# Scattering one expert's output in eight pieces between the next expert's products, and the rotary key's low part as two zero-padded planes

## The chip, the cores and the metric

The kernel runs on one core of a Trainium2 chip. The metric is the device time of one execution in microseconds (us); the time of a version is the median of its runs. One execution is also recorded by the profiler; its span runs from the first to the last instruction.

## The reference

One layer of a transformer block on 512 tokens of width 1024, all in f32:

```python
h   = rmsnorm(x) * (1 + sc1) + sh1                       # shift and scale from a condition vector
c_q, c_kv, k_pe, dil, gates = split(h @ w_in)
o_a = mla_attention(...)     # 8 heads; score = q_nope . k_nope (128 wide) + q_pe . k_pe (64 wide, rotary, one key for all heads)
o_b = dilated_band_attention(...)                        # 3 groups of 8 heads, softmax-weighted
x   = x + gt1 * ((g_a * o_a + g_b * o_b) @ w_out)
h2  = rmsnorm(x) * (1 + sc2) + sh2
aff = softmax(h2 @ w_router)                             # 16 experts
gate, idx = top_k(aff.T, 64)                             # each expert chooses 64 tokens
for each expert e:
    xe  = h2[idx[e]]                                     # 64 x 1024
    ye  = (silu(xe @ w_gate[e]) * (xe @ w_up[e])) @ w_down[e] * gate[e]     # 1024 -> 2048 -> 1024
    out[idx[e]] += ye
x   = rmsnorm(x + gt2 * out)
```

The three matrices of an expert hold 2048 x 1024 f32 each, 8.4 MB; the 16 experts' weights are read once.

## The kernel before

All is one function, `tile_block`. Each engine has its own list of instructions and runs it in order; V is VectorE (DVE), A is ScalarE (ACT), G is GpSimd (POOL), T is TensorE (PE), SP issues nearly all transfers. The program states tiles and operations; a planner (`TileContext(nc, schedule_with_timeline_sim=True)`) sets the order in each list, by the order of the source, but with ready work put ahead where it reckons that an engine would stand still. It adds the waits. A tile name with `bufs=n` has n buffers; a new tile of the name waits until the oldest has been read for the last time. Pools that are closed give their room to later pools, whose first writes wait for the last readers of that room.

Precise products are made from two halves: `split` writes a rounded f32r high part (ACT) and the rest as a low part (DVE, L415 and L416), and three products high x high, high x low, low x high are summed (`TERMS`).

The stages, in order of time:

- Preparation and the projections of the low-rank attention (0 to 126 us). `kr` holds the rotary key: 128 partitions, where two copies of its 64 rows lie one above the other, and two planes, high and low. `ltm`, two 128x128 triangular masks for ranking tokens, is copied here from the masks' tile (L332), and `c32`, the condition vector repeated 32 times, is made here.
- Low-rank attention (126 to 273 us). For each of 4 pairs of heads and 4 blocks of 128 queries, each head's 128x512 scores are five products (L656 to L661): three of `q_` and `k_`, one of `qr` and the high plane of `kr` over 128 rows, and one over 64 rows: `qr` holds a head's query, high part in one half of the partitions and low part in the other, and only the half `r_` with the high part meets the low plane of the key:

```python
T.matmul(pp[hh_], qr[hh_][:, qs], kr[:, 0], start=False, stop=False)           # L660
T.matmul(pp[hh_], qr[hh_][r_, qs], kr[r_, 1], start=False, stop=True)          # L661
```

  Between them lie table lookups (`lookup`, L306 to L330) for the other attention's biases, through DRAM.
- Dilated attention, output projection and routing logits (273 to 921 us), `route` at the end.
- Ranking: the top 64 tokens of each expert (921 to 938 us), mostly on DVE; `ltm` is used at L1055. `onesb` (L1002) is the first tile of the ranking's pool.
- The experts (938 to 1905 us), below, then the last additions, the final norm and the store.

For the experts the weights come through a ring of nine 2 MB buffers (`we`, `RING`). Each expert takes 12 loads: four of `w_gate` and four of `w_up` in turn, each 2 of the 8 blocks of 128 rows, then four of `w_down`. They are issued by SP in that order, each when the buffer that it takes has been read. The last expert's `w_down` comes in smaller column pieces (L990), and one buffer of the ring is used there for the final gains.

For expert e the source goes in this order: `gw`, the one-hot selection of 64 tokens twice side by side (DVE, L1096); `px`, the gathered rows as a product with it (L1101); `xe`, four transposes and scaling to `xT` (L1104 to L1111); transposes of `gw` into `se`, the scatter matrix (L1115, L1117); the gate values `gv` as sums over tokens (L1120); `pg` and `pu`, the products with `w_gate` and `w_up` in four chunks each (L1134); silu and multiplication to `hid` (L1139, L1140), transposed to `hT` (L1143, L1144); `py`, the product with `w_down` (L1151); `yf` and `ye`, scaled and split into high and low (L1155 to L1160); and the scatter: 8 times a product of `se` and `ye` of 512 columns (L1164), added to `x1` by DVE (L1166). `px`, `pg`, `pu` and `py` have 64 rows of output each, in two halves of the 128 partitions side by side ("128*64" in the rows); transposes, sums and scatters use 128 ("128*128").

PSUM has 8 banks: `px` 1, `pg` 2, `pu` 2, `py` 1, and two buffers of `tpb`, which the transposes, the sums and the scatters share.

Of the kernel before, what the change touches and what calls it, by code (L numbers as in the profile page):

```python
# [101 lines left out]
def tile_block(ctx, tc, x, c, positions, w_ada, b_ada, g_norm_mix, w_in, g_q_lat, g_kv_lat, w_uq, w_ukv,  # L102
# [23 lines left out]
    V.memset(one_c, 1.0)  # L126
    a2c = per.tile([P, KD], F32, name="a2c")
    sh2c = per.tile([P, KD], F32, name="sh2c")
    ltm = per.tile([P, 2, P], BF16, name="ltm")

    def axb(E, out_, a, s_, b, op0, op1, t):

# [22 lines left out]
    with ExitStack() as pa:  # L155
# [173 lines left out]
            SP.dma_start(bias_d[u].rearrange("h (a e) k -> a h (e k)", a=16),  # L329
                         stage_d[u].rearrange("(a h) n -> a h n", a=16))  # L330

        V.tensor_copy(ltm, mk[:, M_LT:M_LT + 256].rearrange("p (a n) -> p a n", a=2))  # L332


        th = wk.tile([P, KD], F32, name="cth")
        A.activation(th, cc, AF.Tanh, scale=0.5)
        V.scalar_tensor_tensor(th, th, 1.0, cc, op0=OP.add, op1=OP.mult)
        c32 = hp.tile([P, KD, 32], F32, name="c32")
        V.tensor_scalar(c32, th[:, :, None].to_broadcast([P, KD, 32]), 0.5, None, op0=OP.mult)
        gmix = wk.tile([P, KD], F32, name="gmix")  # L340
        glat = lp.tile([P, 5], F32, name="glat")
# [2 lines left out]
        def ada_step(g, k):  # L344

            load_ada(g, k)
            wt = w_ada_t[g, k]
            if k:
                V.scalar_tensor_tensor(wt, wt, c32[:, k, 0:1], w_ada_t[g, k - 1], op0=OP.mult, op1=OP.add)
            else:  # L350
                V.tensor_scalar(wt, wt, c32[:, k, 0:1], None, op0=OP.mult)

        def ada(g):

# [177 lines left out]
            V.tensor_mul(dst, src, cos)  # L532
            V.tensor_add(dst, dst, t)

        kr = lp.tile([P, 2, S], F32R, name="kr")
        roped(kpe, kpe)
        split(kr, kpe)
        bp_.close()

        st_.close()  # L540
# [94 lines left out]
        for pr_ in range(H // 2):  # L635
            q_, k_, qr, wv4 = cur
            if pr_ == 0:
                vv = values(wv4)
            pT = {}

            def attend(jp):

                po = pj().rearrange("p (h q) -> p h q", h=2)
                for hh_ in range(2):
                    sums(po[:, hh_], [(lambda a, k=k: vv[:, a, k, 128 * hh_:128 * hh_ + 128],
                                       lambda b, k=k: pT[jp, hh_][:, b, k]) for k in range(NT)])
                A.copy(y[:, 2 * pr_:2 * pr_ + 2, 256 * jp:256 * jp + 256], po)

            for j in range(NT):
                place()  # L650
                if j % 2 == 0:
                    for hh_ in range(2):
                        pT[j // 2, hh_] = wk.tile([P, 2, NT, 256], F32R, name="pT", bufs=PTB)
                qs = slice(128 * j, 128 * j + 128)
                pp = [sc(), sc()]
                for hh_ in range(2):  # L656
                    r_ = slice(64 * hh_, 64 * hh_ + 64)
                    for n, (a, b) in enumerate(TERMS):
                        T.matmul(pp[hh_], q_[hh_][:, a, qs], k_[hh_][:, b], start=n == 0, stop=False)  # L659
                    T.matmul(pp[hh_], qr[hh_][:, qs], kr[:, 0], start=False, stop=False)  # L660
                    T.matmul(pp[hh_], qr[hh_][r_, qs], kr[r_, 1], start=False, stop=True)  # L661
                for hh_ in range(2):
                    st4 = wk.tile([P, 4], F32, name="st4", bufs=4)
                    V.reduce_max(st4[:, 0:1], pp[hh_], axis=AX.X)
                    V.tensor_scalar(st4[:, 1:2], st4[:, 0:1], nrs[:, j:j + 1], None, op0=OP.mult)
                    n_pe[0] += 1
                    pe = x1[:, 2 + n_pe[0] // 2 % 2, 512 * (n_pe[0] % 2):512 * (n_pe[0] % 2) + 512]
                    A.activation(pe, pp[hh_], AF.Exp, bias=st4[:, 1:2], scale=prs[:, j:j + 1], accum_out=st4[:, 2:3])
                    V.reciprocal(st4[:, 3:4], st4[:, 2:3])
                    V.tensor_scalar(pe, pe, st4[:, 3:4], None, op0=OP.mult)  # L670
                    pt = tp()
                    for k in range(NT):
                        T.transpose(pt[:, 128 * k:128 * k + 128], pe[:, 128 * k:128 * k + 128], ident)
                    split(pT[j // 2, hh_][:, :, :, 128 * (j % 2):128 * (j % 2) + 128],
                          pt.rearrange("p (k q) -> p k q", k=NT))
                if j == PVJ:
                    attend(0)
                if j == RJ and pr_ < H // 2 - 1:
                    ahead = rope_queries(pr_ + 1)
            if pr_ < H // 2 - 1:  # L680
                cur = project(*ahead)
            attend(1)
            if pr_ < H // 2 - 1:
                vv = values(cur[3])
# [313 lines left out]

        loaded = [weights(0, n) for n in range(len(RING))]

        onesb = wk.tile([P, P], BF16, name="onesb")
        G.memset(onesb, 1.0)  # L1002
        spare = y.rearrange("p h s -> p (h s)")[:, 3 * D:]
# [67 lines left out]
    with ExitStack() as pb_:  # L1071
# [4 lines left out]
        for dh in range(2):  # L1076
            SP.dma_start(gt2[64 * dh:64 * dh + 64],
                         mod_d[5 * D + 512 * dh:5 * D + 512 * dh + 512].unsqueeze(0).to_broadcast([64, 512]))
        for e in range(E_N):
            wl = []  # L1080
            for n in range(12):
# [8 lines left out]
                wl.append(loaded.pop(0) if loaded else weights(e, n))  # L1090
            wg, wu = ([w_.rearrange("p (r f) -> p r f", r=2) for w_ in wl[i:8:2]] for i in range(2))
            wd = [w_.rearrange("p (r d) -> p r d", r=4) for w_ in wl[8:]]

            gw = wbs.tile([P, NT, 2, CAP], F32, name="gw", bufs=1)
            for j in range(NT):
                V.tensor_scalar(gw[:, j], iota[:, None, :].to_broadcast([P, 2, CAP]), pos[:, j, e:e + 1], None,  # L1096
                                op0=OP.is_equal)
            px = ps.tile([P, 512], F32, name="px", bufs=1)
            for j in range(NT):
                for dh in range(2):  # L1100
                    T.matmul(px[64 * dh:64 * dh + 64], gw[:, j, 0], xn[:, j, 512 * dh:512 * dh + 512],  # L1101
                             start=j == 0, stop=j == NT - 1)
            xe = wbs.tile([P, 4, P], F32, name="xe", bufs=1)
            V.tensor_copy(xe, px.rearrange("q (p r) -> q r p", r=4))  # L1104
            pt = ps.tile([P, 512], F32, name="tpb", bufs=2)
            for n in range(4):
                T.transpose(pt[:, 128 * n:128 * n + 128], xe[:, n], ident)
            xT = wbs.tile([P, KD, CAP], F32, name="xT", bufs=2)
            V.tensor_tensor(xT.rearrange("p (h n) s -> p n h s", h=2), pt.rearrange("p (n h s) -> p n h s", n=4, h=2),
                            a2c.rearrange("p (h n) -> p n h", h=2)[:, :, :, None].to_broadcast([P, 4, 2, CAP]), op=OP.mult)  # L1110
            V.tensor_tensor(xT, xT, sh2c[:, :, None].to_broadcast([P, KD, CAP]), op=OP.add)  # L1111

            pt = ps.tile([P, 512], F32, name="tpb", bufs=2)
            for j in range(NT):
# [6 lines left out]
                         start=j == 0, stop=j == NT - 1)  # L1121
            gv = wbs.tile([P, 1], F32, name="gv", bufs=2)
            V.tensor_copy(gv, pt[:, 0:1])

            pg = ps.tile([P, 2, 512], F32, name="pg", bufs=1)
            pu = ps.tile([P, 2, 512], F32, name="pu", bufs=1)
            for c in range(4):
                for w_, acc in ((wg[c], pg), (wu[c], pu)):
                    for r in range(2):
                        k = 2 * c + r  # L1130
                        for b in range(2):
                            for hf in range(2):
                                f0 = 1024 * b + 512 * hf
                                T.matmul(acc[64 * hf:64 * hf + 64, b], xT[:, k], w_[:, r, f0:f0 + 512],  # L1134
                                         start=k == 0, stop=k == KD - 1)
            hid = wbs.tile([P, 2, 4, P], F32, name="hid", bufs=1)
            hT = wbs.tile([P, 4, 4, CAP], F32, name="hT", bufs=1)
            for b in range(2):
                A.activation(hid[:, b], pg[:, b].rearrange("q (p r) -> q r p", r=4), AF.Silu)  # L1139
                V.tensor_mul(hid[:, b], hid[:, b], pu[:, b].rearrange("q (p r) -> q r p", r=4))  # L1140
                pt = ps.tile([P, 512], F32, name="tpb", bufs=2)
                for n in range(4):
                    T.transpose(pt[:, 128 * n:128 * n + 128], hid[:, b, n], ident)  # L1143
# [4 lines left out]
            for g in range(4):  # L1148
                for r in range(4):
                    for dh in range(2):  # L1150
                        T.matmul(py[64 * dh:64 * dh + 64], hT[:, g, r], wd[g][:, r, 512 * dh:512 * dh + 512],  # L1151
                                 start=g == 0 and r == 0, stop=g == 3 and r == 3)

            yf = wbs.tile([P, 512], F32, name="yf", bufs=1)
            V.scalar_tensor_tensor(yf, py, gv, gt2, op0=OP.mult, op1=OP.mult)  # L1155
            ye = wbs.tile([P, 2, 512], F32R, name="ye", bufs=1)
            for dh in range(2):
                r_, o_ = slice(64 * dh, 64 * dh + 64), slice(64 - 64 * dh, 128 - 64 * dh)
                A.activation(ye[r_, dh], yf[r_], AF.Copy)
                V.tensor_sub(ye[o_, dh], yf[r_], ye[r_, dh].bitcast(F32))  # L1160
            for dh in range(2):
                for j in range(NT):
                    pt = ps.tile([P, 512], F32, name="tpb", bufs=2)
                    T.matmul(pt, se[:, j], ye[:, dh], start=True, stop=True)  # L1164
                    ds_ = slice(512 * dh, 512 * dh + 512)
                    V.tensor_add(x1[:, j, ds_], x1[:, j, ds_], pt)  # L1166


        ssf = wbs.tile([P, NT, 3], F32, name="ssf")
# [70 lines left out]
```

## Time and profile before

| | |
|---|---|
| runs | 1934.15, 1939.73, 1940.28 us; median 1939.73 |
| profiled execution | 1937.67 us; span 1935.9 us |
| mean granted TensorE clock | 0.926 of full speed |
| busy share of the span | PE 92%, PE weight loads 55%, DVE 38%, ACT 20%, POOL 8% |
| moved from HBM | 520 MB read, 277 GB/s read and written over the span |

The page gives busy time by engine, the span in 40 slices of 48.4 us with busy tenths, granted clock and DMA share, and the chain of work that ended last. That chain says which instruction, or wait, each stretch of time is owed to. Matmuls are pipelined and their ends are modelled, so the duration of one matmul is longer than the distance to the next; in the chain the rows give the distance.

### The profile page before, as it was taken

To read this page: it belongs to the slowest core of one execution; us is meant where nothing else is said; L and a number is where in the kernel's file an instruction comes from. 1 tells how busy PE (TensorE), PEld (TensorE's weight loads), DVE (VectorE), ACT (ScalarE), POOL (GpSimd) and SP (SyncE) were. 2 spreads that over 40 slices of the span, in tenths; PEclk is the share of its full clock that TensorE was granted. 3 is DMA by queue.
4 is the path that set the end of the run, shared out by engine and by line. 5 is a ranking of instruction groups with operands and counts; after the bars stand their busy time and mean duration, and the time that the engine had idled before them with its cause. 6 is when DMAs were issued, how large, how long until landed. Compare 5 with 4: busy or idle time off the path is not lost.

```text
span 1935.9 us, 21457 instructions
## 1 busy us (share of the span) xinstructions
PE 1777.8 (92%) x8812; PEld 1058.4 (55%) x8812; DVE 739.9 (38%) x1384; ACT 395.4 (20%) x769; POOL 156.0 (8%) x140
## 2 busy tenths in 40 slices
PE   4699999999999999999699999999999999999995
PEld 1466667888888888888233333334333343333332
DVE  6567865556454354445322022211222012220213
ACT  2345643322232322333000000000000000000002
POOL 6710000020020020010200000000000000000002
PEclk7799999999999999999799988899888988889888
DMA  8346666535533234234799999999999999999983
GB/s 268 92 134 212 220 200 199 154 121 154 179 102 119 66 88 122 88 109 177 312 428 427 419 407 406 399 429 403 404 403 424 407 406 406 405 429 405 406 355 93
DMA packets 133537, 531.20 MB, mean 274 GB/s; under 512 B 16952, under 2 KB 93880, under 8 KB 105792
## 3 DMA queue, kind: packets, MB, share of 16 engines
q1 hardware_dynamic: 131360, 523.02, 70.4%
q0 software_dynamic: 2080, 6.82, 0.9%
q8 instruction: 69, 1.13, 0.2%
q14 instruction: 28, 0.23, 0.0%
HBM read 520.45 MB, written 16.17 MB: 277 GB/s over the span
## 4 chain that ended last, share of the span: by engine, by line
PE 84%; DVE 8%; DMA 3%; ACT 2%; issue 2%; SPq 1%; ACTq 0%; DVEq 0%
PE pj L459 20%; PE pg L1134 13%; PE pu L1134 11%; PE py L1151 11%; PE pj L813 5%; PE pj L554 3%; PE px L1101 3%; PE tpb L1164 2%; PE sc L554 2%; DVE x L1166 2%; PE sc L884 1%; PE tpb L1120 1%; DMA raw<-in_w_ada_dram 1%; PE sc L659 1%; DMA y<-in_x_dram 1%
## 5 line engine op out<-in xcount | busy, mean ns | idle before, releaser
L459 PE MATMUL pj<-hh,ws 128*128 128x512 f32 x1248 | 406.4, 401 | 13.7 <-ACT ws L415 8.4
L459 PEld LDWEIGHTS pj<-hh,ws 128*128 128x128 f32 x1248 | 235.7, 189 | 74.4 <-ACT ws L415 8.6
L1134 PE MATMUL pg<-we,xT 128*64 128x512 f32 x1024 | 267.4, 655 | 0.0
L459 PE MATMUL pj<-hl,ws 128*128 128x512 f32 x624 | 249.7, 400 | 3.2 <-DVE hl L449 3.2
L1134 PE MATMUL pu<-we,xT 128*64 128x512 f32 x1024 | 237.3, 592 | 0.0
L1151 PE MATMUL py<-we,hT 128*64 128x512 f32 x960 | 209.3, 594 | 2.6 <-ACT hT L1144 1.1
L416 DVE TENSOR_TENSOR ws<-raw,ws 128x1024 fp32r<-128x1024 f32 (+2 forms) x114 | 141.0, 1239 | 146.7 <-ACT ws L415 146.2
L415 ACT ACTIVATE ws<-raw 128x1024 fp32r<-128x1024 f32 (+2 forms) x114 | 117.0, 1030 | 272.2 <-PE pj L459 188.6
L1134 PEld LDWEIGHTS pg<-we,xT 128*64 128x64 f32 x1024 | 86.2, 151 | 151.8 <-issue 151.5
L1134 PEld LDWEIGHTS pu<-we,xT 128*64 128x64 f32 x1024 | 83.1, 137 | 137.9 <-issue 137.6
L1151 PEld LDWEIGHTS py<-we,hT 128*64 128x64 f32 x960 | 67.6, 137 | 134.6 <-issue 128.5
L459 PEld LDWEIGHTS pj<-hl,ws 128*128 128x128 f32 x624 | 118.1, 189 | 30.5 <-DVE hl L449 3.9
L1164 PE MATMUL tpb<-ye,se 128*128 128x512 f32 x120 | 76.8, 726 | 49.5 <-DVE ye L1160 35.8
L1140 DVE TENSOR_TENSOR hid<-hid,pu 128x512 f32<-128x512 f32 x32 | 20.6, 684 | 243.5 <-PE pu L1134 243.5
L1139 ACT ACTIVATE hid<-pg 128x512 f32<-128x512 f32 x32 | 17.4, 594 | 470.1 <-PE pg L1134 470.1
L1104 DVE COPY xe<-px 128x512 f32<-128x512 f32 x16 | 11.1, 692 | 259.0 <-PE px L1101 259.0
L1155 DVE SCALAR_TENSOR_TENSOR yf<-py,gv,gt 128x512 f32<-128x512 f32 x15 | 11.3, 751 | 221.6 <-PE py L1151 221.6
L813 PE MATMUL pj<-ws,hh 128*128 128x256 f32 x512 | 94.4, 282 | 0.0
L1164 PEld LDWEIGHTS tpb<-ye,se 128*128 128x128 f32 x120 | 31.5, 275 | 100.4 <-issue 59.1
L1166 DVE TENSOR_TENSOR x<-x,tpb 128x512 f32<-128x512 f32 x120 | 78.0, 685 | 14.9 <-PE tpb L1164 13.5
L813 PEld LDWEIGHTS pj<-ws,hh 128*128 128x128 f32 x512 | 79.3, 188 | 0.0
L1101 PE MATMUL px<-xn,gw 128*64 128x512 f32 x256 | 75.8, 613 | 2.0 <-DVE gw L1096 2.0
(331 smaller groups left out, 1941.1 us busy)
## 6 DMA issues: line engine op xcount, KB each, us to landing
we<-in_w_gate_dram SPq DMA_DIRECT2D x64, 2048.0 KB, 15.6
we<-in_w_up_dram SPq DMA_DIRECT2D x64, 2048.0 KB
we<-in_w_down_dram SPq DMA_DIRECT2D x60, 2048.0 KB, 9.3
raw<-in_w_in_dram SPq DMA_DIRECT2D x38, 1024.0 KB, 5.3
raw<-in_w_ada_dram SPq DMA_DIRECT2D x22, 1024.0 KB, 6.9
x<-bkt_d SPq DMA_DIRECT2D x104, 128.0 KB, 4.1
raw<-in_w_in_dram SPq DMA_DIRECT2D x16, 512.0 KB, 5.3
stage_d<-stage POOLq DMA_DIRECT2D x26, 256.0 KB, 4.9
```

The source lines that it names most:

```text
L415: A.activation(dst[:, 0], src, AF.Copy)
L416: V.tensor_sub(dst[:, 1], src, dst[:, 0].bitcast(F32))
L459: T.matmul(pu, parts[k // 4][:, a, k % 4, col:col + 128], hx[b][:, k], start=k == 0 and n == 0, stop=k == KD - 1 and n == 2)
L554: T.matmul(out_, w_(a), b_(b), start=i == 0, stop=i == n_ - 1)
L659: T.matmul(pp[hh_], q_[hh_][:, a, qs], k_[hh_][:, b], start=n == 0, stop=False)
L813: T.matmul(pu[:, 256 * j:256 * j + 256], hx[b][:, k, 128 * m:128 * m + 128], parts[k // 4][:, a, k % 4], start=k == 0 and n == 0, stop=k = ...
L1101: T.matmul(px[64 * dh:64 * dh + 64], gw[:, j, 0], xn[:, j, 512 * dh:512 * dh + 512], start=j == 0, stop=j == NT - 1)
L1134: T.matmul(acc[64 * hf:64 * hf + 64, b], xT[:, k], w_[:, r, f0:f0 + 512], start=k == 0, stop=k == KD - 1)
L1140: V.tensor_mul(hid[:, b], hid[:, b], pu[:, b].rearrange("q (p r) -> q r p", r=4))
L1151: T.matmul(py[64 * dh:64 * dh + 64], hT[:, g, r], wd[g][:, r, 512 * dh:512 * dh + 512], start=g == 0 and r == 0, stop=g == 3 and r == 3)
L1164: T.matmul(pt, se[:, j], ye[:, dh], start=True, stop=True)
L1166: V.tensor_add(x1[:, j, ds_], x1[:, j, ds_], pt)
```

## The change

Two things, with small moves that make room for them.

The scatter of expert e no longer stands at the end of its own pass. Its eight products and additions stand in the pass of expert e + 1, one behind each chunk of `pg` and of `pu`. The transposes of `gw` and the sums for `gv` go behind the products. The next expert's selection and gather (`select`, `gather`) stand between `hid` and its transposes, and the transposes of the gathered rows (`rows`) behind the first quarter of `py`. The first expert has its own ahead of the loop. The last expert's own scatter, which was a separate piece of code, stays as it is.

`kr` gets three planes: the high part, and two low planes with the lower part in one half of the partitions and zeros in the other. The 64-row product becomes one over 128 rows. The zeros are written by GpSimd; the low part is made by two subtractions of 64 partitions.

`ltm` moves to the ranking's pool and is loaded there by a transfer that ACT issues; `c32` moves to a pool that closes earlier, and `ada_step` reads the condition vector from `cc`, which is overwritten with its silu.

```diff
-    ltm = per.tile([P, 2, P], BF16, name="ltm")
-        V.tensor_copy(ltm, mk[:, M_LT:M_LT + 256].rearrange("p (a n) -> p a n", a=2))
...
-        c32 = hp.tile([P, KD, 32], F32, name="c32")
+        V.tensor_scalar(cc, th, 0.5, None, op0=OP.mult)
+        c32 = wk.tile([P, KD, 32], F32, name="c32")
...
-        kr = lp.tile([P, 2, S], F32R, name="kr")
+        kr = lp.tile([P, 3, S], F32R, name="kr")
+        for u in range(2):
+            G.memset(kr[64 - 64 * u:128 - 64 * u, 1 + u].bitcast(F32), 0.0)
         roped(kpe, kpe)
-        split(kr, kpe)
+        A.activation(kr[:, 0], kpe, AF.Copy)
+        for u in range(2):
+            r_ = slice(64 * u, 64 * u + 64)
+            V.tensor_sub(kr[r_, 1 + u], kpe[r_], kr[r_, 0].bitcast(F32))
...
-                    T.matmul(pp[hh_], qr[hh_][r_, qs], kr[r_, 1], start=False, stop=True)
+                    T.matmul(pp[hh_], qr[hh_][:, qs], kr[:, 1 + hh_], start=False, stop=True)
...
+        ltm = wk.tile([P, 2, P], BF16, name="ltm")
+        A.dma_start(ltm.rearrange("p a n -> p (a n)"), masks[:, M_LT:M_LT + 256])
...
+        def select(e): ...      # gw
+        def gather(e, gw): ...  # px
+        def rows(px): ...       # xe, its transposes, xT
+        def scatter(se, ye, j, dh):
+            pt = ps.tile([P, 512], F32, name="tpb", bufs=2)
+            T.matmul(pt, se[:, j], ye[:, dh], start=True, stop=True)
+            ds_ = slice(512 * dh, 512 * dh + 512)
+            V.tensor_add(x1[:, j, ds_], x1[:, j, ds_], pt)
         for e in range(E_N):
...
+            if e == 0:
+                gw = select(0)
+                xT = rows(gather(0, gw))
+            for c in range(4):
+                for i, (w_, acc) in enumerate(((wg[c], pg), (wu[c], pu))):
+                    ...                                  # 8 products
+                    if e:
+                        scatter(se, ye, c, i)
...                                                       # gw transposes to se, gv
...                                                       # hid for b in 0, 1
+            if e < E_N - 1:
+                gw = select(e + 1)
+                px = gather(e + 1, gw)
+            for b in range(2):
...                                                       # hid transposes, hT
...                                                       # py for g in range(4), and in it
+                if g == 0:
+                    xT = rows(px)
...                                                       # yf, ye
-            for dh in range(2):
-                for j in range(NT):
-                    pt = ps.tile([P, 512], F32, name="tpb", bufs=2)
-                    T.matmul(pt, se[:, j], ye[:, dh], start=True, stop=True)
-                    ds_ = slice(512 * dh, 512 * dh + 512)
-                    V.tensor_add(x1[:, j, ds_], x1[:, j, ds_], pt)
```

More of the change, by code (lines that the diff above doesn't have):

```diff
@@ L348, in ada_step @@
             if k:
-                V.scalar_tensor_tensor(wt, wt, c32[:, k, 0:1], w_ada_t[g, k - 1], op0=OP.mult, op1=OP.add)
+                V.scalar_tensor_tensor(wt, wt, cc[:, k:k + 1], w_ada_t[g, k - 1], op0=OP.mult, op1=OP.add)
             else:
-                V.tensor_scalar(wt, wt, c32[:, k, 0:1], None, op0=OP.mult)
+                V.tensor_scalar(wt, wt, cc[:, k:k + 1], None, op0=OP.mult)
         def ada(g):
@@ L656, in tile_block @@
                 for hh_ in range(2):
-                    r_ = slice(64 * hh_, 64 * hh_ + 64)
                     for n, (a, b) in enumerate(TERMS):
@@ L1078, in tile_block, with select, gather, rows @@
                          mod_d[5 * D + 512 * dh:5 * D + 512 * dh + 512].unsqueeze(0).to_broadcast([64, 512]))
+        def select(e):
+            gw = wbs.tile([P, NT, 2, CAP], F32, name="gw", bufs=1)
+            for j in range(NT):
+                V.tensor_scalar(gw[:, j], iota[:, None, :].to_broadcast([P, 2, CAP]), pos[:, j, e:e + 1], None,
+                                op0=OP.is_equal)
+            return gw
+        def gather(e, gw):
+            px = ps.tile([P, 512], F32, name="px", bufs=1)
+            for j in range(NT):
+                for dh in range(2):
+                    T.matmul(px[64 * dh:64 * dh + 64], gw[:, j, 0], xn[:, j, 512 * dh:512 * dh + 512],
+                             start=j == 0, stop=j == NT - 1)
+            return px
+        def rows(px):
+            xe = wbs.tile([P, 4, P], F32, name="xe", bufs=1)
+            V.tensor_copy(xe, px.rearrange("q (p r) -> q r p", r=4))
+            pt = ps.tile([P, 512], F32, name="tpb", bufs=2)
+            for n in range(4):
+                T.transpose(pt[:, 128 * n:128 * n + 128], xe[:, n], ident)
+            xT = wbs.tile([P, KD, CAP], F32, name="xT", bufs=2)
+            V.tensor_tensor(xT.rearrange("p (h n) s -> p n h s", h=2), pt.rearrange("p (n h s) -> p n h s", n=4, h=2),
+                            a2c.rearrange("p (h n) -> p n h", h=2)[:, :, :, None].to_broadcast([P, 4, 2, CAP]), op=OP.mult)
+            V.tensor_tensor(xT, xT, sh2c[:, :, None].to_broadcast([P, KD, CAP]), op=OP.add)
+            return xT
+        def scatter(se, ye, j, dh):
+            pt = ps.tile([P, 512], F32, name="tpb", bufs=2)
+            T.matmul(pt, se[:, j], ye[:, dh], start=True, stop=True)
+            ds_ = slice(512 * dh, 512 * dh + 512)
+            V.tensor_add(x1[:, j, ds_], x1[:, j, ds_], pt)
         for e in range(E_N):
@@ L1092, in tile_block @@
             wd = [w_.rearrange("p (r d) -> p r d", r=4) for w_ in wl[8:]]
-            gw = wbs.tile([P, NT, 2, CAP], F32, name="gw", bufs=1)
-            for j in range(NT):
[L1096 to L1099, printed above, removed]
-                for dh in range(2):
[L1101 to L1104, printed above, removed]
-            pt = ps.tile([P, 512], F32, name="tpb", bufs=2)
[L1106 to L1111, printed above, removed]
+            if e == 0:
+                gw = select(0)
+                xT = rows(gather(0, gw))
+            pg = ps.tile([P, 2, 512], F32, name="pg", bufs=1)
+            pu = ps.tile([P, 2, 512], F32, name="pu", bufs=1)
+            for c in range(4):
+                for i, (w_, acc) in enumerate(((wg[c], pg), (wu[c], pu))):
+                    for r in range(2):
+                        k = 2 * c + r
+                        for b in range(2):
+                            for hf in range(2):
+                                f0 = 1024 * b + 512 * hf
+                                T.matmul(acc[64 * hf:64 * hf + 64, b], xT[:, k], w_[:, r, f0:f0 + 512],
+                                         start=k == 0, stop=k == KD - 1)
+                    if e:
+                        scatter(se, ye, c, i)
             pt = ps.tile([P, 512], F32, name="tpb", bufs=2)
@@ L1123, in tile_block @@
             V.tensor_copy(gv, pt[:, 0:1])
[L1125 to L1135, printed above, removed]
             hid = wbs.tile([P, 2, 4, P], F32, name="hid", bufs=1)
@@ L1140, in tile_block @@
                 V.tensor_mul(hid[:, b], hid[:, b], pu[:, b].rearrange("q (p r) -> q r p", r=4))
+            if e < E_N - 1:
+                gw = select(e + 1)
+                px = gather(e + 1, gw)
+            for b in range(2):
                 pt = ps.tile([P, 512], F32, name="tpb", bufs=2)
@@ L1160, in tile_block @@
                 V.tensor_sub(ye[o_, dh], yf[r_], ye[r_, dh].bitcast(F32))
[L1161 to L1164, printed above, removed]
-                    ds_ = slice(512 * dh, 512 * dh + 512)
-                    V.tensor_add(x1[:, j, ds_], x1[:, j, ds_], pt)
         ssf = wbs.tile([P, NT, 3], F32, name="ssf")
```

## The prediction

> **What bounds the kernel now.** I read the page's slices first, then busy time by stretches, then the chain that ended last.
>
> ```profile
> DMA  8346666535533234234799999999999999999983
> ```
>
> From slice 20 on (950 us, the experts) the DMA engines are full or nearly. Stretches of that stage (columns: stretch, length, busy us of PE, PEld, DVE, ACT, POOL with counts, granted clock, DMA share, GB/s):
>
> ```profile
> 960.00:1060.00 100.00, 92.39 (x409) 33.49 (x405) 20.49 (x35) 7.42 (x13) 0.00 (x0) 0.94 1.01 428
> 1240.00:1250.00 10.00, 9.24 (x26) 5.60 (x28) 6.79 (x15) 0.59 (x1) 0.00 (x0) 0.50 1.00 428
> 1250.00:1260.00 10.00, 10.00 (x40) 3.05 (x38) 0.00 (x0) 0.00 (x0) 0.00 (x0) 0.83 0.75 288
> 951.00:1895.00 944.00, 879.06 (x3717) 348.22 (x3714) 174.56 (x313) 61.70 (x107) 2.45 (x4) 0.90 0.97 408
> 1870.00:1895.00 25.00, 24.14 (x115) 7.86 (x112) 1.03 (x2) 1.08 (x2) 0.00 (x0) 1.00 0.98 336
> ```
>
> PE is busy 879 of 944 and the DMA share is 0.97. A full stream moves 428 GB/s; each expert has one hole (0.75, 288) and, just before it, the clock at 0.50. The chain shows what PE does there, from one expert's last product to the next expert's first ones (start, length, what):
>
> ```profile
> 1222.38 13.98 PE py L1151 x64
> 1236.39 0.76 DVE yf L1155
> 1237.23 0.64 ACT ye L1159
> 1237.89 0.68 DVE ye L1160
> ...
> 1240.90 0.70 DVE x L1166
> 1241.73 0.78 PE tpb L1164
> ...
> 1245.96 0.85 PE tpb L1115 x4
> 1246.82 1.80 PE tpb L1120 x8
> 1248.61 6.02 PE pg L1134 x16
> 1254.63 3.43 PE pu L1134 x16
> ```
>
> Between 1236.36 and 1248.61 PE has 12.25 us of scatter chain, transposes and column sums; it cools, so the first chunk of `pg` takes 6.02 instead of 3.43. No weight slot is released from 1236.4 to 1254.6, the ring of nine runs full, and the queue stands still. So the order on PE sets the end here, and the stream is only 3% behind it: 408 against 428.
>
> **The scatter part: what PE needs.** Products, 8 chunks x 3.43 = 27.4. Scatters, 8 a 512-column fp32r matmul (0.23, row L660 below) plus going from the 128x64 tiling to 128x128 and back. No row shows that pair; the nearest are a one-third-column matmul group among full ones and a 64-row matmul among full ones:
>
> ```profile
> 160.57 1.41 PE tp L324 x24
> 172.15 0.76 PE tp L324 x12
> 184.93 0.70 PE sc L659 x3
> 185.63 0.23 PE sc L660
> 185.86 0.42 PE sc L661
> 186.28 0.89 PE sc L659 x3
> ```
>
> Twelve more of L324 cost 0.65, so 12 at 0.76 hold 0.11 for the visit. L661 takes 0.19 more than L660, and the three behind it 0.19 to 0.20 more than 0.70: 0.39. A visit costs 0.11 to 0.39; I take 0.39, since a scatter changes a full 128-column weight as L661 does. Eight scatters: 0.62 x 8 = 5.0 (2.7 at the other end; below nothing is excluded, it is added work on PE).
> The first scatter stands 3.43 behind the last `py`. Its `ye` needs 0.76+0.64+0.68 and hops, 2.2, the other half 2.9: no wait, 0.5 to spare. Queued behind it is `pu` of the first chunk, and through it the slot release. Each add on DVE (0.70) has a chunk's time, and two `tpb` buffers suffice.
> After the products come the `gw` transposes (0.85) and sums. Warm sums cost 1.05, as in the first expert:
>
> ```profile
> 946.40 1.05 PE tpb L1120 x8
> 947.45 3.58 PE pg L1134 x16
> 1203.78 1.29 PE px L1101 x6
> 1221.00 0.67 PE tpb L1143 x4
> 1221.75 0.59 ACT hT L1144
> ```
>
> They cover the `hid` chain; the next `select` (4 x 0.215 on DVE) stands behind two `hid` multiplies, so `px` starts some 2.65 after the last `pu`, runs 3.43 (16 x 0.215 by the x6 row), then 0.67 and 0.59 until `py`: 7.5 in all. `py` with the `xe` transposes inside (13.98 + 0.67 + 0.39): 15.0; `xT` is ready 10 us before it is wanted. Then the next `pg` at once, warm, 0.2. Sum: 27.4 + 5.0 + 7.5 + 15.0 + 0.2 = 55.1 per expert (52.8 at the cheap end). Today's first `pg` chunks stand 947.45 to 1864.50, over 15 experts 61.1 each.
>
> **What the stream needs.** 0.408 x 944 = 385.2 MB. The last expert's `w_down` (2048 x 1024 x 4 bytes = 8.4 MB, in shorter rows) at 336: 25.0. The other 376.8 MB at 428: 880.4. Together 905.4 instead of 944; a full expert's 25.2 MB (three such matrices) take 58.8. PE's 55.1 is below that, so what was PE's order becomes the stream. SP keeps its order; it waits for slots that are freed in the same order, one every 4.1 instead of 3.43 in the products. The longest stretch without release is 7.5 + 3.4 = 10.9, 2.2 loads; by then 8 releases less 5.8 loads leave 2.2 outstanding in the first expert: it just holds, and I add 2 us.
>
> The start and the end, by engine rows:
>
> ```profile
> 951.08 7.19 SPq L996 DMA_DIRECT2D we<-in_w_down_dram  x3
> 1864.50 5.32 PE L1134 MATMUL pg<-we,xT 128*64 128x512 f32 x16
> 1910.12 1.95 PE L1182 MATMUL py<-we,hT 128*64 128x256 f32 x16
> 1914.12 1.08 PE L1182 MATMUL py<-we,hT 128*64 128x256 f32 x8
> ```
>
> In the first expert `gv` no longer stands ahead of `pg`, which then waits for `xT`: 0.4 earlier, the stream starts at 950.6 and ends at 1856.0 + 2. Its last piece has one x16 group of products behind it, 1.95: 1860. From there to the end now: 1915.2 to the span's 1935.9, 20.7, work that the change leaves alone. 1880.7 for the scatter part: 55 us less. Today PE reaches that point 20 us behind the last landing; most of that lag goes too, since PE then waits for each landing.
> PE would be the later one if its period P put 947 + 15 P + 76 (the last expert, 1864.5 to 1935.9, plus scatters and sums) beyond 1880.7: from P = 57.2. The margin is 2 us an expert.
>
> **The key part.** 32 matmuls like L661 become like L660: 32 x 0.39 = 12.5 if PE paces the scores.
>
> ```profile
> L661 PE MATMUL sc<-kr,qr x32: 490/495/503, 131.1 to 272.8; 64*128 64x512 f32 x32
> 126.00:273.00 147.00, 140.94 (x923) 96.41 (x921) 116.00 (x239) 86.55 (x170) 15.55 (x26) 1.00 0.70 222
> DVE x L320 <- DMA x<-bkt_d: 22.4, 14, 5.0
> 128.42 0.69 DVE L591 TENSOR_TENSOR qr<-qp,qr 64x512 fp32r<-64x512 f32 x1
> 126.54 1.35 POOL L328 DMA_DIRECT2D stage_d<-stage  x2 [24.19 <-ACT stage L327]
> 916.33 0.20 POOL L1002 MEMSET onesb<- 128x128 bf16 x1 [23.80 <-PE sc L554]
> 934.71 0.11 PEld L1055 LDWEIGHTS <-ltm 128*128 128x128 bf16 x1
> ```
>
> PE is busy 141 of 147, but the table lookups hold DVE for 22.4 of it, so I count 0.83: 10.4 (0 to 12.5). Added: the low part as two half-height subtractions, one more of 0.69 on a DVE that is busy there: 0.7. The two memsets lie in POOL's 24 us of idling; uncovered, about 1. The products read the zero rows at no extra columns.
> `ltm` now comes by a DMA on ACT's queue. Like `onesb` it needs the room that L554 frees at 916.3; behind it wait ACT's copies for the last routing block, at most 0.7 + 0.4 of issue, I take 0.3. Its landing has until 934.7. The early copy of `ltm` (0.3) and the new small write of `cc` cancel. Net of this part: 9.4.
>
> **Sum.** Span 1880.7 - 9.4 = 1871.3. The profiled execution took 1937.67 for a span of 1935.9, and the median of the runs, 1939.73, stands 2.1 above it: 1871.3 + 1.8 + 2.1 = 1875.
>
> **One rule against the change.** The visit to the other tiling is between 0.11 and 0.39 in the rows above. The Trainium skill, "TensorEngine Tiling (Array Packing)", section Key Properties, says that changing the tiling mode drains TensorE, and gives no price; L661 agrees with a drain of 0.2 a side. It speaks for the key part and against eight scatters strewn among 64-column products.
>
> **Rivals.**
> *PE stays the later one.* The planner puts ready work where it likes (today `px` stands between chunks of `pg` and `pu`, row 1203.78), so scatters may bunch on two `tpb` buffers at 0.78 each, or `px` wait for `select`. For it: 2 us of margin; against: every wait above has cover. P = 57.5 to 60.5 gives 1023 + 15 P - 9.4 + 3.9: 1880 to 1925, at 59 1902.
> *Slower: the drain.* If each of the 16 switches per expert costs c in place of 0.2, P = 52.0 + 16 c; it decides where 1023 + 15 P - 5.5 passes 1939.7, P = 61.5 or c = 0.59, three times the row's value, and at c = 0.8 gives 1990. For it: no row has this very switch; against: both near rows. This is the page's rule taken at a high price.
> *It doesn't do what it says.* The planner pulls the scatters back behind `py`, and the lookups pace the scores: 1935 to 1943. Against: `pg`'s first chunk is ready at `py`'s end.
> *The stream at another rate.* The stretch that the sum uses shows 428; 1.5% either way, as a guess at how it varies, takes 13 off or adds 13.
>
> **How the numbers follow.** Stream-bound 0.66, own range 1858 to 1892; PE later 0.22; no change 0.05; drain 0.07. A change under 0.3% cannot be told from none here (the three runs spread 0.3%). Faster 0.88, same 0.05, slower 0.07. Range: 1858 to take the rate and the keys at their best, 1908 to take in two thirds of the PE case.
>
> **What would show it.** DMA share 1.00 and about 428 GB/s in every full 10 us from 960 to 1830; clock near 1.00 there; PE waiting on `we` by DMA, which today's waits do not list; L1164-like scatters one by one behind chunks; scores without the 0.42 row; the last 21 us unchanged. I am wrong if the hole per expert stays, if PE never waits for weights, or if the scatters' visits take over 0.4.

## The result, and the profile after

| | before | changed |
|---|---|---|
| median of the runs | 1940.01 us (4 runs, those beside the changed kernel among them, 1934.15 to 1940.90) | 1883.61 us (4 runs, 1881.46 to 1887.84) |
| profiled execution, its span | 1937.67, 1935.9 us | 1885.46, 1883.7 us |
| mean granted TensorE clock | 0.926 | 0.973 |

The ratio of the changed kernel to the one before is 0.9718, with a 95% interval of 0.9691 to 0.9745: 56 us less. 1875 was predicted, with a range of 1858 to 1908; the measured time is 8.6 above the point and inside the range.

The slices of the span from the page (granted clock in tenths, DMA share in tenths, GB/s):

```profile
PEclk7799999999999999999899999999999999999998
DMA  9346766535534233231879999999999999999996
GB/s 270 91 124 196 249 195 192 179 107 152 176 112 126 90 90 104 90 88 70 363 322 427 427 428 427 428 428 428 427 428 427 427 428 427 428 427 428 427 424 205
```

From slice 22 to slice 39 the stream stands at 424 to 428 GB/s without a break. The same by stretches of time, with the columns of the prediction's table (stretch, length, busy us of PE, PEld, DVE, ACT, POOL, clock, DMA share, GB/s):

```profile
1240.00:1250.00 10.00, 10.00 (x50) 3.36 (x48) 0.00 (x0) 0.46 (x1) 0.00 (x0) 1.00 1.01 426
1250.00:1260.00 10.00, 9.01 (x46) 3.38 (x44) 1.83 (x3) 1.76 (x4) 0.00 (x0) 1.00 1.01 431
960.00:1830.00 870.00, 799.99 (x3638) 281.14 (x3636) 172.90 (x311) 60.72 (x105) 2.43 (x4) 1.00 1.01 427
1834.00:1859.00 25.00, 21.85 (x120) 8.84 (x118) 5.83 (x10) 5.15 (x12) 3.11 (x3) 1.00 0.97 338
126.00:273.00 147.00, 134.91 (x926) 100.39 (x926) 116.55 (x241) 85.76 (x171) 14.86 (x26) 0.98 0.71 223
```

Before, twelve of the sixteen experts had a 10 us stretch with a share of 0.75 to 0.87, and the one ahead of it had a clock of 0.50 to 0.71. Neither is there now: 1.01 and 1.00 over the whole 870 us, and in its single stretches of 10 us a share of 0.99 to 1.03 and a clock of 1.00 but for two (0.91 and 0.92, from 1280 to 1300). The last expert's short rows run at 338, taken as 336.

From the chain that ended last, between one expert's `py` and the next expert's products (start, length, what):

```profile
1194.69 3.46 PE pu L1148 x16
...
1198.24 0.70 DVE hid L1168
...
1200.37 3.65 PE py L1183 x16
1204.03 0.59 PE tpb L1108 x4
1204.62 10.45 PE py L1183 x48
1215.07 3.43 PE pg L1148 x16
1218.50 0.45 PE tpb L1117
...
1218.97 1.29 DVE x L1119 x2
...
1220.31 0.50 PE tpb L1117
1220.81 3.58 PE pu L1148 x16
1224.39 0.45 PE tpb L1117
...
1226.70 3.58 PE pg L1148 x16
1230.29 0.59 PE tpb L1155 x4
1230.88 0.80 PE tpb L1160 x8
```

`py` ends at 1215.07 and the next `pg` begins there, at 3.43 for its first chunk, where it took 6.02 after 12.25 us of other work. The scatters, however, do not stand one behind each chunk. The planner has put four behind the first chunk and four behind the second; each four take 2.31 us (1218.50 to 1220.81), most of it two additions on DVE that free the two `tpb` buffers. Most passes look much like this one. In two passes of the same chain the price of one visit shows. In the second expert's pass the scatters stand one by one, most of them inside a chunk; in the third's, two stand behind a whole chunk with both buffers free:

```profile
1016.65 2.57 PE pu L1148 x10
1019.21 0.43 PE tpb L1117
1019.65 1.86 PE pu L1148 x6
1021.51 0.42 PE tpb L1117
...
1058.88 0.66 PE tpb L1117 x2
1059.54 3.58 PE pg L1148 x16
```

The eight chunks and eight scatters of the second expert take 35.4 us (995.46 to 1030.81), 7.9 more than eight chunks of 3.43: 0.99 a scatter, or 0.76 beyond the 0.23 of its product. The two together cost 0.66 and 0.15 in the chunk behind them, 0.35 beyond their products.

PE now waits for weights; the list of waits before has no such row. Between 940 and 1850 us (total, times, longest):

```profile
PE py L1183 <- DMA we<-in_w_down_dram: 18.1, 17, 2.1
...
PE pg L1148 <- DMA we<-in_w_gate_dram: 13.6, 11, 1.3
...
PE pu L1148 <- DMA we<-in_w_up_dram: 5.1, 7, 1.2
```

The starts of `yf`, one for each expert but the last, give the period (here the first, the fifth to seventh and the fifteenth):

```profile
995.51 0.75 DVE L1189 SCALAR_TENSOR_TENSOR yf<-py,gv,gt 128x512 f32<-128x512 f32 x1 [9.04 <-PE py L1183]
...
1215.11 0.75 DVE L1189 SCALAR_TENSOR_TENSOR yf<-py,gv,gt 128x512 f32<-128x512 f32 x1 [9.04 <-PE py L1183]
...
1269.92 0.75 DVE L1189 SCALAR_TENSOR_TENSOR yf<-py,gv,gt 128x512 f32<-128x512 f32 x1 [9.04 <-PE py L1183]
...
1328.20 0.75 DVE L1189 SCALAR_TENSOR_TENSOR yf<-py,gv,gt 128x512 f32<-128x512 f32 x1 [9.86 <-PE py L1183]
...
1801.20 0.75 DVE L1189 SCALAR_TENSOR_TENSOR yf<-py,gv,gt 128x512 f32<-128x512 f32 x1 [11.06 <-PE py L1183]
```

At first PE sets the pace and eats into the loads that were made ahead: 1269.92 - 1215.11 = 54.8. (The first period, with the scatters one by one, is 56.5; the next four are 54.1 to 54.8.) From the seventh expert on the stream does: (1801.20 - 1328.20) / 8 = 59.1. A full expert's 25.2 MB at 427 GB/s take 59.0.

The start, from the chain and then from the rows of SP's queue (the first load for which a buffer had to come free):

```profile
939.48 5.65 PE px L1098 x16
...
947.41 1.05 PE tpb L1160 x8
948.46 3.58 PE pg L1148 x16
```

```profile
952.08 0.33 SPq L1000 DMA_DIRECT2D we<-in_w_down_dram  x1
```

And the last score products, by line (min, median, max ns, first and last start):

```profile
L665 PE MATMUL sc<-kr,qr x32: 387/393/632, 132.2 to 272.6; 128*128 128x512 f32 x32
```

The 64-row product of 495 ns is now one of 393. Yet the last one starts at 272.6, against 272.8 before, and the stream starts at 952.08, against 951.08. In these 147 us PE is busy 6.0 us less than before (134.91, after 140.94), but it only waits longer, at a mean clock of 0.98 after 1.00. From the first of these products to the last it takes 140.4 us, where it took 141.7.

### The profile page after: what moved, and what is told of

The parts are those of the page before. It is cut to its first block, busy times and chain, and to the rows that moved or that the text cites. A ratio compares the mean times of both kernels' runs of the same rounds, so it can differ in the third digit from the quotient of the medians.

```text
span 1883.7 us, 21450 instructions
## 1 busy us (share of the span) xinstructions
PE 1711.5 (91%) x8812; PEld 1001.6 (53%) x8812; DVE 738.6 (39%) x1385; ACT 394.3 (21%) x769; POOL 155.9 (8%) x142
## 4 chain that ended last, share of the span: by engine, by line
PE 62%; DMA 25%; DVE 6%; issue 4%; SPq 1%; ACT 1%; POOL 0%; ACTq 0%; DVEq 0%; POOLq 0%
PE pj L458 21%; DMA we<-in_w_gate_dram 12%; DMA we<-in_w_up_dram 9%; PE pu L1148 8%; PE pg L1148 8%; PE pj L817 5%; PE py L1183 4%; PE px L1098 2%; PE sc L559 2%; DVE x L1119 2%; PE pj L559 2%; PE sc L888 2%; PE tpb L1117 1%; DMA x<-bkt_d 1%; DMA raw<-in_w_ada_dram 1%
## 5 line engine op out<-in xcount | busy, mean ns | idle before, releaser
L1148 PE MATMUL pg<-we,xT 128*64 128x512 f32 x1024 | 233.4, 595 | 14.4 <-DMA we<-in_w_gate_dram 13.6
L1183 PE MATMUL py<-we,hT 128*64 128x512 f32 x960 | 216.3, 597 | 20.0 <-DMA we<-in_w_down_dram 18.1
L1148 PEld LDWEIGHTS pg<-we,xT 128*64 128x64 f32 x1024 | 73.0, 137 | 156.0 <-issue 130.9
L1148 PEld LDWEIGHTS pu<-we,xT 128*64 128x64 f32 x1024 | 72.2, 137 | 147.7 <-issue 134.0
L1168 DVE TENSOR_TENSOR hid<-hid,pu 128x512 f32<-128x512 f32 x32 | 20.6, 684 | 219.6 <-PE pu L1148 219.6
L1193 ACT ACTIVATE ye<-yf 64x512 fp32r<-64x512 f32 x30 | 18.8, 628 | 252.1 <-DVE yf L1189 251.7
L817 PE MATMUL pj<-ws,hl 128*128 128x256 f32 x256 | 71.6, 280 | 0.0
L1098 PE MATMUL px<-xn,gw 128*64 128x512 f32 x256 | 61.3, 613 | 5.1 <-DVE gw L1090 5.1
```

The costliest lines, as they stand in the source:

```text
L817: T.matmul(pu[:, 256 * j:256 * j + 256], hx[b][:, k, 128 * m:128 * m + 128], parts[k // 4][:, a, k % 4], start=k == 0 and n == 0, stop=k = ...
```

## The experiments

Two theories stood: the expert stage is bound by PE's order before and by the stream after, and nothing of the gain is in the keys, because the score stage waits for something other than PE. The rivals were that the key part carries part of the gain, that the placing of the scatters in the source is what opened the hole, and that PE still paces the experts.

**One part alone.** `e1_scatter_only` is the changed kernel with the old two-plane key, `e2_key_only` the kernel before with the three-plane key and the moves of `ltm` and `c32`.

```diff
 e1, from the changed kernel
-kr = lp.tile([P, 3, S], F32R, name="kr")
+kr = lp.tile([P, 2, S], F32R, name="kr")
-T.matmul(pp[hh_], qr[hh_][:, qs], kr[:, 1 + hh_], start=False, stop=True)
+T.matmul(pp[hh_], qr[hh_][r_, qs], kr[r_, 1], start=False, stop=True)
 e2, from the kernel before: the same lines the other way
```

> The changed kernel with the key part undone: `kr` in two planes and the 64-row product again; the moved scatter and the moves of `ltm` and `c32` stay. Theory (the whole gain is the expert stage's, which now runs at the rate of the weight stream): 1879 to 1886 us, the same as the changed kernel's 1883.6, with the first `pg` within 1.5 us of 948.4. Rival (the key part gained what was forecast and the rest of the change gave it back before the experts): about 9 us slower than the changed kernel, 1893.

> The kernel before with the key part and the moves of `ltm` and `c32`, the expert loop as before. Theory (the score stage is not paced by PE, so the freed PE time turns into waits): 1938 to 1942 us, no change from 1940; PE busy in 126 to 273 us down by 6 us and the stage as long as before. Rival (the key part is worth 9 us by itself): 1931.

Measured: e1 1883.81, ratio 0.9723 (0.9708 to 0.9738), the same as with both parts. Its first `pg` was expected within 1.5 us of 948.4 and stands at 945.8, earlier without the key part. e2 1935.86, ratio 0.9988 (0.9976 to 1.0000): at most a few us, though the time itself lies below what was expected, and PE's busy time in the score stage fell by 8.5, not 6. So, to within a few us, the gain comes from the expert stage. The last score product starts at 271.5 in e1 and at 274.1 in e2, against 272.6 in the changed kernel and 272.8 before. The new key products end the stage no earlier in either pair.

**What the score stage waits for.** Between 126 and 273 us the kernel before had 4.9 us of PE waiting for DVE, most of it in two rows:

```profile
PE tp L673 <- DVE pT L416: 2.4, 1, 2.4
...
PE tp L324 <- DVE x L320: 1.9, 2, 1.2
```

In the changed kernel it is 10.0, while DVE itself waits for the table loads as long as before (22.4):

```profile
DVE x L319 <- DMA x<-bkt_d: 21.8, 13, 4.9
PE tp L323 <- DVE x L319: 4.8, 4, 2.0
PE tp L677 <- DVE pT L415: 3.3, 1, 3.3
```

SP issues the table loads, and also the copy of each finished bias (L328). The suspicion was that this copy, waiting for its own input, holds the loads behind it in SP's queue. Two kernels have that one word changed:

```diff
-SP.dma_start(bias_d[u].rearrange("h (a e) k -> a h (e k)", a=16),
+G.dma_start(bias_d[u].rearrange("h (a e) k -> a h (e k)", a=16),
```

> The changed kernel with one word changed in the table lookups: the copy of a finished table from `stage_d` to `bias_d` is issued by GpSimd and no longer by SP, where it waits for the stage transfer to land ahead of the next lookup's loads. Theory (that wait in SP's queue paces the score stage and hides the key part): the score stage shortens, up to 12 us, and the time falls to 1871 to 1879. Rival (DVE, or the loads' own landing, paces the stage): 1881 to 1886, no change.

> The kernel before with the same one word: the copy from `stage_d` to `bias_d` is issued by GpSimd. Theory (with 64-row products PE itself takes 141 of the stage's 147 us, so the freed queue can give at most 6): 1934 to 1940. If the theory of e3 holds, the gap between e3 and e4 is larger than that between the changed kernel and the one before (56) by 4 to 12 us. Rival (the queue has nothing to do with it): 1938 to 1942 and a gap of 56.

Measured: e3 1880.48 (0.9700, interval 0.9686 to 0.9714), e4 1937.11 (0.9992, 0.9980 to 1.0004). In e3 the last score product starts at 268.9, 3.7 earlier, and the wait for the tables falls from 21.8 to 17.0:

```profile
DVE x L319 <- DMA x<-bkt_d: 17.0, 13, 4.1
```

In five traces with the new key and the copy on SP that product starts at 272.1 to 274.1, so the 3.7 are more than their spread. The queue is a part of it, 3 to 5 us, not the whole; up to 12 had been expected. In time e3 stands 3 us below the changed kernel with overlapping intervals, which is not enough to call it a gain: it misses the theory's 1871 to 1879, and the gap between e4 and e3 is 56.6, as the rival had it.

So two more leave the loads of 24 of the 26 lookups out (96 of 104 transfers); those lookups work on what their buffers hold. Each was run once.

```diff
-for s_ in range(4):
+for s_ in range(4 if n_look[0] <= 2 else 0):
```

> The changed kernel without the table loads after the first two: the lookups compare, multiply and store as before, but on what lies in their buffers. This leaves out 24 of 26 loads of table indices. Theory (the score stage waits for these loads, and that hid the key part): the last score product ends by 262 instead of 273 us, PE idle in the stage under 3 us. Rival (DVE or the planner's order paces the stage): ends at 270 to 273.

> The kernel before, likewise without the table loads after the first two (24 of 26 left out). Theory (with the loads out of the way the stage is paced by PE, and the 64-row products cost 0.39 each): the last score product ends 9 to 13 us later than in e11, at 270 to 273. Rival (the key part has no worth even then): within 3 us of e11.

The line of the last score product and the stretch of the score stage, for e11 (changed) and then for e12 (before):

```profile
L665 PE MATMUL sc<-kr,qr x32: 387/395/400, 132.1 to 256.9; 128*128 128x512 f32 x32
```

```profile
126.00:273.00 147.00, 144.96 (x1018) 112.36 (x1018) 122.22 (x256) 89.54 (x179) 16.55 (x27) 1.00 0.48 155
```

```profile
L661 PE MATMUL sc<-kr,qr x32: 491/497/502, 130.8 to 265.4; 64*128 64x512 f32 x32
```

```profile
126.00:273.00 147.00, 146.67 (x961) 102.69 (x960) 121.90 (x250) 88.58 (x177) 16.94 (x26) 1.00 0.43 143
```

PE is busy 145 and 147 of the 147, and now the last score product starts at 256.9 with the new key and at 265.4 with the old: 8.5 earlier, just under the 9 to 13 that were expected. From the first of these products to the last it is 124.8 against 134.6, which makes 0.31 us for each of the 32. The first `pg` follows, 930.8 against 938.7. e11 was to end by 262 and did; e12 was to end at 270 to 273 and ended before 266. The saving in PE's work is real, and with the loads in place it is lost in waits. The loads also bind first: without them the old key's stage ends 7.4 earlier (265.4 for 272.8), while the new key alone ends it no earlier. Against the changed kernel, e11's first `pg` is 17.6 earlier and its time 15.8 shorter (1867.83): what the start gains the end gains nearly in full.

**Who paces the experts.** Two kernels give PE more work, eight extra matmuls in each gather whose sums the real gather then overwrites (1.72 us):

```diff
+for j in range(2):
+    for dh in range(2):
+        T.matmul(px[64 * dh:64 * dh + 64], gw[:, j, 0], xn[:, j, 512 * dh:512 * dh + 512],
+                 start=j == 0, stop=j == 1)
```

> The changed kernel with eight more gather matmuls per expert: the first half of `px` is computed once ahead of the real one, 8 x 0.215 = 1.72 us of PE time per expert, 27.5 over 16. Theory (the weight stream paces the experts, PE has slack: unhindered it takes 54.1 to 54.8 us per expert against the stream's 58.8): 1881 to 1889 us, nothing or a few us. Rival (PE's order still paces the experts): 1911.

> The kernel before with the same eight more gather matmuls per expert. Theory (there PE's order paces the experts): about 27 us more than 1939, 1960 to 1970. Rival (the stream paced that kernel as well): 1936 to 1944.

Two others take a twelfth of the stream away from experts 1 to 14: the first quarter of `w_down` is filled with 0.01 by GpSimd, not loaded, and its products are made from that.

```diff
-SP.dma_start(w_, w_down[0, e, k:k + 512, :].rearrange("(p r) d -> p (r d)", p=P))
+if n == 8 and e > 0:
+    G.memset(w_, 0.01)
+else:
+    SP.dma_start(w_, w_down[0, e, k:k + 512, :].rearrange("(p r) d -> p (r d)", p=P))
```

> The changed kernel with the first quarter of `w_down` of experts 1 to 14 not loaded but set to a constant by GpSimd: 14 x 4.9 = 69 us less of the stream. This leaves out a twelfth of those experts' weights. Theory (stream-paced at 58.8 per expert, with PE's own 54.5 next): PE paces, about 14 x 4.3 = 60 us less from the stream but no earlier than 948.4 + 15 x 54.5 + 76 = 1842 us of span: 1838 to 1852. Rival (something else than the stream paces it): 1880 to 1886.

> The kernel before with the same quarter of `w_down` not loaded but set by GpSimd (a twelfth of the weights of experts 1 to 14 left out). Theory (PE's order paces that kernel, the stream has slack): 1930 to 1941, nothing or a few us less. Rival (the stream paced it): 1870 to 1880.

| | from the changed kernel | from the kernel before |
|---|---|---|
| 1.72 us more on PE per expert | e5 1886.58, +3 | e6 1948.78, +10 |
| a twelfth of the stream less | e7 1844.42, -39 | e8 1922.94, -16 |

Each is set against its own parent. The kernel before, run beside them, took 1939.21; their ratios to it are 0.9730 (0.9683 to 0.9777), 1.0048 (1.0005 to 1.0092), 0.9513 (0.9485 to 0.9540) and 0.9918 (0.9889 to 0.9946), in the order e5, e6, e7, e8. So e5 cannot be told from the changed kernel, and the other three moved. The changed kernel hardly minds more work on PE and gains much from a shorter stream, as the theory has it; the kernel before loses by the one and gains less than half as much by the other. In e5 the early periods, after a first of 58.3, rise to 55.0 to 56.5, and the later ones stay at 58.5 to 59.9, the stream's. In e7 the stream no longer sets the pace, and PE's own period shows in the starts of `yf`, 54.9 apart:

```profile
1218.06 0.75 DVE L1192 SCALAR_TENSOR_TENSOR yf<-py,gv,gt 128x512 f32<-128x512 f32 x1 [9.04 <-PE py L1186]
...
1272.96 0.75 DVE L1192 SCALAR_TENSOR_TENSOR yf<-py,gv,gt 128x512 f32<-128x512 f32 x1 [9.04 <-PE py L1186]
```

Two sizes were missed, and the chains show why. Take the fifteen passes from the first `pg` to the last expert's first `pg`, and cut each into the first chunk of `pg`, the way from there to `py`, and the way from the start of `py` to the next `pg` (sums in us):

| | first chunks | to `py` | `py` to the next `pg` | all |
|---|---|---|---|---|
| before | 80.8 | 442.8 | 393.6 | 917.1 |
| e6 | 74.2 | 467.6 | 387.3 | 929.1 |
| e8 | 77.1 | 436.0 | 389.4 | 902.5 |

e6 was expected to lose 27 and lost 9.6. The added work stands in its chain nearly whole (24.8 of 15 x 1.72 = 25.8, on the way to `py`). What hides half of it is that the first chunks and the chain behind `py` run faster, 6.5 and 6.3, at a mean clock of 0.942 where the kernel before had 0.925 to 0.928 beside it. From e6's chain, at the start of the sixth expert's products:

```profile
1255.60 4.97 PE pg L1138 x16
```

The first `pg` chunk takes 4.97 here, where it took 6.02. e8 was expected to gain up to 9 and gained some 16: 1.9 ahead of the first `pg` and 14.6 in these passes. This is not the stream's doing by any wait that shows: the waits of e8, as those of the kernel before, have no row of PE waiting for weights. The planner made another order for it. In twelve of its passes `px` stands whole between the last `pu` and the transposes of `hid`, where PE would wait, and the way to `py` takes some 28.9; before, it stands so in four, and in the others that way takes some 29.8. Some first chunks and chains behind `py` are also faster, at a mean clock of 0.933. So e8 is no clean test of the stream's share in the kernel before.

**Where the scatters stand.** This kernel is the changed one with the scatters at the end of their own pass, as before. Selection, gather, `rows`, and the `gw` transposes and sums stay at their new places.

```diff
-                    if e:
-                        scatter(se, ye, c, i)
 after ye:
+            for dh in range(2):
+                for j in range(NT):
+                    scatter(se, ye, j, dh)
```

> The changed kernel with the eight scatters back at the end of their own expert's pass, and all else as changed (selection, gather and transposes of the next expert ahead, sums behind the products). Theory (the scatter chain is what leaves PE idle and cold): PE's 54.5 less 5 for the interleaved scatters plus some 8.5 for the chain behind `py` and 2.6 for a cold first chunk, 60.6 per expert: PE paces again, 1925 to 1940 us. Rival (it was the other moves, the transposes and sums taken out from between the experts, that opened the way): at or under 58.8 per expert, 1881 to 1895.

Measured: 1884.25, ratio 0.9730 (0.9709 to 0.9751). The theory, 1925 to 1940, fell: the time is that of the changed kernel. From its chain:

```profile
1214.01 3.43 PE pg L1148 x16
1217.44 0.45 PE tpb L1117
...
1217.91 1.30 DVE x L1119 x2
...
1219.26 0.50 PE tpb L1117
1219.75 3.58 PE pu L1148 x16
```

The planner puts four scatters behind the first chunk and four behind the second all the same. It can, because the next expert's `xT` is ready long before `py` ends (the `xe` transposes stand inside `py`, at 1204.03 in the changed kernel), so that ready products stand there when `py` is done. Before, those transposes came after the scatters in the source and shared two `tpb` buffers with them, and the column sums came too: nothing of the next expert but `px` went ahead. So the gain is that of the moved preparation, selection to `xT` and the `gw` transposes and sums. That the order and the shared buffers were what held it back is read from the source and the chain; which of these moves would do alone was not tried.

**A version with both ends trimmed.** `e10_pool_bias_and_warm` is e3 with eight more matmuls in the ranking, into a buffer that nothing reads, so that the first expert's gather (5.65 us for 16 matmuls, against 3.43) finds a faster clock.

```diff
+if j >= 2:
+    warm = ps.tile([P, 512], F32, name="pj", bufs=2)
+    for n in range(4):
+        T.matmul(warm, ident, xn[:, j, :512], start=n == 0, stop=n == 3)
```

> The changed kernel with the copy to `bias_d` issued by GpSimd (as in e3) and eight dummy products of the identity with `xn` during the ranking, where PE stands still, so that the first gather need not start at half clock. Theory: the stream starts earlier by what the first release gains, 3 us from the tables and up to 2.5 from the gather: 1877 to 1880 us, 0.2% to 0.4% under the changed kernel. Rival (the dummies delay the ranking's own products, or the clock falls again by 938 us): as e3, 1880, or slower.

Measured: 1882.02 (1879.05 to 1886.33), ratio 0.9721 (0.9700 to 0.9742). From the first `px` to the first `pg` it takes 6.9 us (935.6 to 942.5) against 9.0 (939.48 to 948.46), but the time is that of the changed kernel within its interval, above the 1877 to 1880 that were expected. Apart from e7 and e11, which leave work out, no version can be told from the changed kernel as faster.

## Why the prediction was right, and where it was not

- **What bounds it.** The hole per expert is gone, the mean clock is 1.00, the stream paces from the seventh expert on: the likeliest case, as forecast. e7 and e5 show it from both sides. That the order on PE was the bound before rests on the waits and the chain; e6 agrees in direction, and e8 cannot decide it.
- **PE's need, 55.1.** e7 measures 54.9, the early experts after the first period 54.1 to 54.8. The sum was right, but with several parts changed, so its closeness is in part luck. The scatters were taken as eight visits of 0.62, 5.0; in most passes they are two groups of 2.31 plus 0.15 more for each chunk behind one (3.58 against 3.43), 4.9. The step from the last `pu` to `py` was taken as 7.5, with `px` behind `select`; `px` is pulled between the chunks, and the two together are 2.22 (1198.15 to 1200.37) and 3.66 (1.94 and 1.72 in the chain behind the rows shown), 5.9. The `gw` transposes and the sums, counted as covered, take 1.8 on PE (1230.29 to 1232.11). `py` with the transposes inside takes 14.7, not 15.0. Together with the 27.4 of products this makes 54.7.
- **The price of a visit, 0.11 to 0.39.** Two scatters behind a whole chunk cost 0.35 for the visit, inside the bracket. The single ones of the second expert cost 0.76 each, outside it, and by the forecast's own sign, over 0.4, it was wrong there; that pass is the period of 56.5. The Trainium skill ("TensorEngine Tiling (Array Packing)", Key Properties) states that changing the tiling mode drains TensorE. These two prices agree with it, though the rows do not tell the drain from the rest of the visit.
- **The planner bunches the scatters.** That stood as the reason for a period of 57.5 to 60.5. The bunching came, and the period did not rise: bunched, they need two visits in place of eight. It was the single visits, which the forecast wanted, that were dear: the period with eight of them was 56.5, still under the stream's 59.1.
- **The stream's need, 905.4 + 2.** From the first release to the last `py` group 909.4 was forecast (1850.6 - 941.2); it took 911.0 (952.08 to 1863.11, the end of the last x8 group). The rate was 427 to 428, and the ring held: no stretch of 10 us shows a share under 0.99. The Trainium skill ("DMA: Bandwidth & Descriptors", Specifications) puts a fabric ceiling at 435 GB/s. The 427 of this trace, over 870 us, come within 2% of it.
- **The end, 20.7.** 1883.7 - 1863.1 = 20.6.
- **The key part, 9.4: the step that failed.** The span was forecast at 1871.3 and is 1883.7. (The median came out only 8.6 above the forecast, since it lies 1.9 below the profiled execution, where it was taken as 2.1 above; that part of the closeness is luck.) Of the 12.4, the stream's start makes 10.9 (952.08 for 941.2), the stream 1.6, the end -0.1. In the start lie the 9.4 of the keys; the 0.4 of `gv`, whose sums the planner still put ahead of the first `pg` (947.41); and 1.1 that the runs' own spread covers (the first `pg` of e1 and e2 stand 2.6 apart). The step went wrong where it multiplied the key products' saving by 0.83, to allow for the lookups' waits on DVE. PE's busy share of 0.96 there was taken for the bound. The lookups' loads were the nearer one: without them alone the stage ends 7.4 earlier, without the key work alone no earlier, since PE then waits 6.0 longer, 5.1 of it for DVE. The saving itself was also put too high, at 0.39 a product; without the loads it is some 0.31. "The lookups pace the scores" had been written down as a rival, with a chance too small for it since it stood there together with the scatters.

## What to carry to other kernels

When a planner orders ready work itself, have the next stage's input ready early; where the pieces in between stand in the source mattered nothing here. That this input should also share no buffer with them is likely, but no run here shows it alone. Such a planner makes a new order for every edit, so a run that is meant to change one resource may change the order as well (as e8): look at its chain before using its time. Once a transfer stream runs without a hole, as here, an earlier first release or fewer bytes make it end earlier, and other work on PE is free up to the stream's period. A busy share of 0.96 does not say that a stage ends by that engine: take the other resource away in a run (as the tables here) before a saving is put in a sum.

## What the runs showed of the hardware

The mean clock was 1.00 over 870 us although PE waited for weights 35 times, 2.1 us at most; two stretches of 10 us show 0.91 and 0.92. Leaving out loads made the kernel before run at a mean clock of 0.933, and giving PE more work at 0.938 to 0.942, after 0.925 to 0.928 beside them. A 512-column scatter between 64-column products cost 0.99 us alone and 0.40 where two stood together behind a whole chunk; a product of that size takes 0.23 in the rows of the score stage.
